# RG-LRU with both directions in one tile, squares on GpSimd, and late gate columns split on GpSimd

## The chip, the cores and the metric

The kernel runs on one core of one Trainium2 chip. The metric is device time in microseconds (us) of one execution; lower is better. The kernel before has a median of 2758.16 us in 3 runs (2757.65 to 2760.92).

## The reference

The program computes two layers (DEPTH = 2) of a hybrid block over 256 context tokens and 512 latent tokens, 1024 channels, in float32. Layer 0 needs all 768 tokens ("full"), layer 1 only the 512 latent ones at its end. One layer, cut to its data flow:

```
h = modulate(rms_norm(x), shift, scale)             # adaLN vectors from c
q, k, v, lx, ly, gdn_qkv, gz, gb, ga, gate = split(h @ w_in)   # 7696 columns
da  = differential attention(q, k, v)               # 4 heads, softmax difference
lru = gelu(ly) * (forward RG-LRU + backward RG-LRU of conv(lx))
gdn = bidirectional gated DeltaNet, chunked
x  += g1 * (sum_i sigmoid(gate_i) * (branch_i @ w_branch_i)) @ w_out
x  += g2 * relu(modulate(rms_norm(x)) @ w1)^2 @ w2
```

The RG-LRU of one direction, which the change touches, is a gated linear scan over time on 512 channels:

```
r, i  = sigmoid(gates of conv(lx))
log_a = -8 * r * softplus(-lam);   a = exp(log_a)
b     = sqrt(-expm1(2 * log_a)) * (i * conv(lx))
h[t]  = a[t] * h[t-1] + b[t]       # direction 1 runs backwards in time
```

## The kernel before

Activations are kept feature-major (128 channels on the partitions, 768 tokens along the free axis). Every large product is done in three passes of a 4-byte type: a weight tile `raw` (128x1024 numbers, 512 KB) is loaded by SyncE's queue, ScalarE copies it rounded to `wh` (the high part), VectorE subtracts to `wl` (the low part, line 174), and TensorE multiplies high by high, high by low and low by high (`mm_feat`, line 201). Three buffers each of `raw`, `wh` and `wl` let the loads run ahead.

A gate column (`fill_gate`, line 863) is one such weight tile: TensorE makes 48 matmuls of it in layer 0 and 24 in layer 1 into one of two large PSUM tiles `pgt`, ScalarE applies a Tanh into `gty`, and the result goes out to HBM. There are 24 gate columns a layer. The first `NG` of them (12 in layer 0, 16 in layer 1) are written in the program ahead of the input projections of the attention and the LRU, the others (12 and 8, here called late) behind the LRU; the scheduler uses them to fill TensorE while other engines work.

The LRU gates are computed earlier and parked in HBM as `lrs[j]`, one tensor for each of four blocks j of 128 channels, with four planes: r of direction 0, i*x of direction 0, r of direction 1, i*x of direction 1. The function `lru` (line 990) takes the blocks in turn. For each direction it loads two planes into a slab `lW` of its own, and calls on ScalarE Exp (a), Tanh (of the same argument, scaled) and Square (a*a); VectorE forms (a*a + 1) * tanh, which is 1 - a*a; ScalarE takes the root, and VectorE or GpSimd multiplies by i*x. Three VectorE scans (forward, backward over the context, backward over the latents) and GpSimd's sum of both directions follow, and a last VectorE product with gelu(ly) (`lys`). ScalarE's calls of `lru` are tied to each other in this order (`behind`), and Exp/Tanh on the one side and Sqrt on the other need different function tables, so an ACT_TABLE_LOAD stands wherever the kind changes.

Behind the LRU come the attention's keys: VectorE writes scaled copies `dkx` (line 1097), TensorE turns them (`pdt`, line 1101), and ScalarE and VectorE split them into `dk`. Then the attention, the merge (`pmf`), the output projection (`pop`) and the MLP (`pm`) follow.

A scheduler places all instructions: it orders each engine's queue before the run, and each engine then works through its own queue in that order. Slabs (11 buffers of 128x3072) are reused as they come free.

Of the kernel before, what the change touches and what calls it, by code (L numbers as in the profile page):

```python
# [22 lines left out]
NG = (12, 16)  # L23
# [5 lines left out]
OFF = {"daq": 0, "dak": 512, "dav": 1024, "lx": 1536, "ly": 2048,  # L29
       "gq": 2560, "gk": 3072, "gv": 3584, "gz": 4096, "ab": 4608, "gate": 4624}  # L30
# [18 lines left out]
def hybrid_prefix_dit_block_kernel(  # L49
# [7 lines left out]
    nc = tc.nc  # L57
    V, S, G, PE = nc.vector, nc.scalar, nc.gpsimd, nc.tensor
# [16 lines left out]
    def slab(name, dt=F32):  # L75
        return sp.tile([P, 3072], dt, name=name, tag="s")
# [48 lines left out]
    for q in range(4):  # L125
        r = slice(32 * q, 32 * q + 16)
# [31 lines left out]
    class Unit:  # L158
        pass

    def wunit(src, early=True):
        u = Unit()
        nk, cols = src.shape[0] // P, src.shape[1]
        with tc.high_priority() if early else nullcontext():
            raw = rp.tile([P, nk, cols], F32, name="raw", tag="raw")
            nc.sync.dma_start(raw, src.rearrange("(k p) c -> p k c", p=P))
            u.h = wp.tile([P, nk, cols], F32R, name="wh", tag="wh")
            u.l = wlp.tile([P, nk, cols], F32R, name="wl", tag="wl")
            u.ins = split(u.h, u.l, raw)
        u.nk = nk  # L170
        return u

    def split(hi, lo, src):
        return S.copy(hi, src), V.tensor_tensor(lo, src, hi.bitcast(F32), op=OP.subtract)  # L174

    class Act:

# [58 lines left out]
    lrs = [dp.tile([P, 4, T], F32, name=f"lrs{i}") for i in range(4)]  # L236
# [626 lines left out]

    def fill_gate(l, L, a, full, n):
        t0, nt = (0, T) if full else (TC, TL)
        us = in_tile(l, OFF["gate"] + P * n)
        ps = big("pgt")
        mm_feat(ps, us, 0, a, pieces(t0, nt))
        y = t3("gty")
        with tc.high_priority():  # L870
            S.activation(y[:, 0:nt], ps[:, 0:nt], AF.Tanh, scale=0.5)  # L871
        nc.sync.dma_start(gts[n][:, t0:T], y[:, 0:nt])
# [32 lines left out]
    def fill_lx_gates(l, L, j, y, weights):  # L905
        wh, wl = weights
        yh, yl = (gp.tile([P, T], F32R, name="gy", tag="g") for _ in range(2))
        parts = ((0, TC, 512, y[:, 0:TC]), (TC, T, 0, y[:, 259:771]))
        for a0, a1, o, src in parts:
            S.copy(yh[:, a0:a1], src)  # L910
            G.tensor_tensor(yl[:, a0:a1], src, yh[:, a0:a1].bitcast(F32), op=OP.subtract)
        for d in range(2):
            for g in range(2):
                ps = big("plg")
                i = 2 * d + g
                for n, (w, x) in enumerate(((wh, yh), (wh, yl), (wl, yh))):
                    for a0, a1, o, src in parts:
                        PE.matmul(ps[:, o:o + a1 - a0], lhsT=w[:, i, :], rhs=x[:, a0:a1], start=(n == 0), stop=(n == 2))
                r = t3("lsg")
                for a0, a1, o, src in parts:  # L920
                    with tc.high_priority():
                        S.activation(r[:, a0:a1], ps[:, o:o + a1 - a0], AF.Tanh, scale=0.5,
                                     bias=L.gb[:, 8 * d + 4 * g + j:8 * d + 4 * g + j + 1])
                    if g == 1:
                        V.scalar_tensor_tensor(r[:, a0:a1], r[:, a0:a1], 1.0, src, op0=OP.add, op1=OP.mult)
                nc.sync.dma_start(lrs[j][:, 2 * d + g, :], r[:, 0:T])

    def fill_ly(l, L, a, full, j):
        t0, nt = (0, T) if full else (TC, TL)
# [65 lines left out]
    def lru(l, L, full, mark):  # L995
        last = [None]
        t0 = 0 if full else TC
        lh = slab("lh").rearrange("p (k t) -> p k t", k=4)

        def act(*args, **kw):  # L1000
            i = S.activation(*args, **kw)
            if last[0] is not None:
                behind(i, last[0])
            last[0] = i

        for j in range(4):
            W = []
            for d in range(2):
                W.append(slab("lW").rearrange("p (k t) -> p k t", k=4))
                after(nc.sync.dma_start(W[d][:, 0:2, :], lrs[j][:, 2 * d:2 * d + 2, :]), mark)  # L1010
            r, ix, at, u = ([W[d][:, i, :] for d in range(2)] for i in range(4))
            for d in range(2):
                c = slice(4 * d + j, 4 * d + j + 1)
                act(at[d], r[d], AF.Exp, scale=L.s8[:, c], bias=L.s8[:, c])
                act(r[d], r[d], AF.Tanh, scale=L.ns8[:, c], bias=L.ns8[:, c])
                act(u[d], at[d], AF.Square)
                V.scalar_tensor_tensor(r[d], u[d], 1.0, r[d], op0=OP.add, op1=OP.mult)
            for d in range(2):
# [323 lines left out]
    for half in range(2):  # L1342
        raws.append([])
        for k in range(8):
# [3 lines left out]
            src = ada_w[0, k * P:(k + 1) * P, 0:2048].rearrange("p (q c) -> p q c", q=2)  # L1348
# [9 lines left out]
    for t in range(6):  # L1358
        xt = xr[t // 3][:, t % 3, :]
        s = slice(t * P, (t + 1) * P)  # L1360
        for hf in range(2):
# [3 lines left out]
            for i in range(4):  # L1365
                n = 4 * hf + i
# [8 lines left out]
    for k in range(8):  # L1375
        i = (G if k % 3 == 1 else V).tensor_tensor(xT[k // 4][:, k % 4, :], x0[k // 4][:, k % 4, :], rb[:, 0:T], op=OP.mult)
# [4 lines left out]
    L = Lay()  # L1381
    spill = [(xs[k // 4][:, k % 4, :], x0[k // 4][:, k % 4, :]) for k in range(8)]
    for l in range(DEPTH):
# [24 lines left out]
        for o in "kvqGLD":  # L1408
# [8 lines left out]
            if o == "L":  # L1417
                lh = lru(l, L, full, R.end)
# [35 lines left out]
        if full:  # L1454
            L = L2
# [36 lines left out]
```

## Time and profile before

| | |
|---|---|
| median of the runs | 2758.16 us |
| profiled execution | 2759.84 us, span 2758.0 us |
| TensorE (PE) busy | 2629.4 us, 95% |
| VectorE (DVE) busy | 1509.1 us, 55% |
| ScalarE (ACT) busy | 1079.5 us, 39% |
| GpSimd (POOL) busy | 456.7 us, 17% |
| share of the chain that ended last | PE 84%, DVE 5%, ACT 5%, issue 3%, DMA 2%, POOL 1% |

How to read it: PE is TensorE's matmuls, PEld its weight loads. The shares are averages over stages that have different limits; a stage has to be read by its own stretch of time. The LRU stage of layer 0 lies at about 600 to 670 us, that of layer 1 at about 2120 to 2185 us. In the rows below, a row of busy times gives the stretch in us, its length, then for each of PE, PEld, DVE, ACT and POOL the busy us and in brackets the number of instructions, then TensorE's granted clock as a share of 2.4 GHz, the DMA engines' share and GB/s. A row of a timeline gives start, duration in us, engine, line, operation, out<-in, shapes, the count that is merged into the row, and in square brackets the idle time before it and what ended it. A row of groups gives line, engine, operation, out<-in and shapes, count, busy us, mean ns of one, and the idle time before.

### The profile page before, as it was taken

To read this page: it belongs to the slowest core of one execution; us is meant where nothing else is said; L and a number is where in the kernel's file an instruction comes from. 1 tells how busy PE (TensorE), PEld (TensorE's weight loads), DVE (VectorE), ACT (ScalarE), POOL (GpSimd) and SP (SyncE) were. 2 spreads that over 40 slices of the span, in tenths; PEclk is the share of its full clock that TensorE was granted. 3 is DMA by queue.
4 is the path that set the end of the run, shared out by engine and by line. 5 is a ranking of instruction groups with operands and counts; after the bars stand their busy time and mean duration, and the time that the engine had idled before them with its cause. 6 is when DMAs were issued, how large, how long until landed. Compare 5 with 4: busy or idle time off the path is not lost.

```text
span 2758.0 us, 44125 instructions
## 1 busy us (share of the span) xinstructions
PE 2629.4 (95%) x17645; PEld 2238.4 (81%) x17645; DVE 1509.1 (55%) x2552; ACT 1079.5 (39%) x1985; POOL 456.7 (17%) x616
## 2 busy tenths in 40 slices
PE   7999999998999989999999989999999798999999
PEld 5788888997888778888888887777897587888887
DVE  6658554459386443333333376686447886544444
ACT  4242454357366233121212253435435764432321
POOL 3001232212012022100001120022222111221100
PEclk9989999999999999999999999999999899999999
DMA  8432233245433643333332222334224533333332
GB/s 277 133 95 88 81 112 102 70 135 182 151 100 104 214 123 115 119 104 122 115 123 77 78 77 70 96 113 148 87 77 129 200 129 120 92 96 99 93 98 77
DMA packets 315588, 318.65 MB, mean 116 GB/s; under 512 B 19500, under 2 KB 268408, under 8 KB 314488
## 3 DMA queue, kind: packets, MB, share of 16 engines
q1 hardware_dynamic: 315384, 315.84, 36.3%
q8 instruction: 139, 2.28, 0.3%
q14 instruction: 65, 0.53, 0.1%
HBM read 259.70 MB, written 56.10 MB: 114 GB/s over the span
## 4 chain that ended last, share of the span: by engine, by line
PE 84%; DVE 5%; ACT 5%; issue 3%; DMA 2%; POOL 1%; SPq 0%; DVEq 0%; ACTq 0%; POOLq 0%
PE pm L201 32%; PE pgt L201 9%; PE pg L201 7%; PE pop L201 4%; PE pqk L218 4%; PE pmf L201 3%; PE pv L218 3%; PE pz L201 2%; PE py L201 2%; PE plx L201 2%; PE pml L201 2%; PE pgd L816 2%; PE ppv L1172 2%; PE pada L347 1%; PE pgd L796 1%
## 5 line engine op out<-in xcount | busy, mean ns | idle before, releaser
L174 ACT CAST wh<-raw 128x1024 fp32r<-128x1024 f32 x288 | 302.3, 1050 | 949.7 <-PE pm L201 616.0
L174 DVE TENSOR_TENSOR wl<-raw,wh 128x1024 fp32r<-128x1024 f32 x288 | 363.8, 1263 | 453.6 <-ACT wh L174 444.8
L201 PE MATMUL pm<-hdh,wh 128*128 128x256 f32 (+1 forms) x896 | 297.4, 332 | 0.4
L201 PE MATMUL pm<-hdl,wh 128*128 128x256 f32 (+1 forms) x896 | 294.5, 329 | 0.0
L201 PE MATMUL pm<-hdh,wl 128*128 128x256 f32 (+1 forms) x896 | 294.3, 328 | 0.0
L1315 DVE SCALAR_TENSOR_TENSOR xT<-pm,mod,xT 128x256 f32<-128x256 f32 (+1 forms) x224 | 133.8, 598 | 236.6 <-PE pm L201 236.6
L201 PE MATMUL pm<-hml,wh 128*128 128x512 f32 (+1 forms) x800 | 244.4, 354 | 5.4 <-DVE hml L459 5.3
L201 PE MATMUL pm<-hmh,wh 128*128 128x512 f32 (+1 forms) x800 | 242.7, 353 | 5.0 <-ACT mr L1296 2.8
L201 PE MATMUL pm<-hmh,wl 128*128 128x512 f32 (+1 forms) x800 | 241.4, 351 | 0.0
L1298 POOL TENSOR_TENSOR mq<-mr 128x768 f32<-128x768 f32 (+1 forms) x64 | 106.5, 1664 | 693.3 <-ACT mr L1296 685.4
L201 PEld LDWEIGHTS pm<-hdh,wh 128*128 128x128 f32 x896 | 170.1, 190 | 30.2 <-DVE xT L1315 7.5
L201 PE MATMUL pgt<-hnh,wh 128*128 128x512 f32 x576 | 177.6, 362 | 7.9 <-ACT gty L871 7.8
L201 PEld LDWEIGHTS pm<-hdh,wl 128*128 128x128 f32 x896 | 170.1, 190 | 15.2
L201 PEld LDWEIGHTS pm<-hdl,wh 128*128 128x128 f32 x896 | 170.2, 190 | 14.8
L201 PE MATMUL pgt<-hnh,wl 128*128 128x512 f32 x576 | 179.7, 364 | 0.0
L201 PE MATMUL pgt<-hnl,wh 128*128 128x512 f32 x576 | 176.7, 361 | 0.0
L201 PEld LDWEIGHTS pm<-hmh,wh 128*128 128x128 f32 x800 | 135.4, 191 | 33.2 <-ACT mr L1296 6.5
L201 PEld LDWEIGHTS pm<-hml,wh 128*128 128x128 f32 x800 | 136.1, 191 | 25.7 <-DVE hml L459 6.2
L201 PEld LDWEIGHTS pm<-hmh,wl 128*128 128x128 f32 x800 | 136.9, 192 | 21.5
L201 PEld LDWEIGHTS pgt<-hnh,wh 128*128 128x128 f32 x576 | 97.2, 193 | 27.0 <-ACT gty L871 10.2
L201 PEld LDWEIGHTS pgt<-hnh,wl 128*128 128x128 f32 x576 | 97.1, 192 | 15.9
L201 PEld LDWEIGHTS pgt<-hnl,wh 128*128 128x128 f32 x576 | 96.2, 191 | 16.0
(427 smaller groups left out, 5963.4 us busy)
## 6 DMA issues: line engine op xcount, KB each, us to landing
raw<-in_mlp_w_dram SPq DMA_DIRECT2D x128, 512.0 KB, 4.1
raw<-in_w_in_dram SPq DMA_DIRECT2D x120, 512.0 KB, 4.1
raw<-in_ada_w_dram SPq DMA_DIRECT2D x80, 512.0 KB, 3.9
lrs<-lsg SPq DMA_DIRECT2D x32, 384.0 KB, 2.4
lW<-lrs SPq DMA_DIRECT2D x16, 768.0 KB, 4.7
raw<-in_w_branch_dram SPq DMA_DIRECT2D x24, 512.0 KB, 4.5
gts<-gty SPq DMA_DIRECT2D x24, 384.0 KB, 2.6
mgg<-gts SPq DMA_DIRECT2D x24, 384.0 KB, 4.2
```

Source lines behind the costliest of these rows:

```text
L174: return S.copy(hi, src), V.tensor_tensor(lo, src, hi.bitcast(F32), op=OP.subtract)
L201: last = PE.matmul(ps[:, o:o + n], lhsT=w, rhs=r[:, t0:t0 + n], start=(k == 0 and i == 0), stop=(k == nk - 1 and i == 2))
L218: PE.matmul(ps[:, 512 * j:512 * j + 256], lhsT=l, rhs=r, start=(k == 0 and i == 0), stop=(k == nk - 1 and i == 2))
L347: i = PE.matmul(ps[32 * q:32 * q + 32, :], lhsT=cact[:, k, :], rhs=two[q // 2][:, 512 * (q % 2):512 * (q % 2) + 512], start=(k == 0), stop ...
L796: i = PE.matmul(dst[32 * h:32 * h + 32, :], lhsT=w, rhs=old[d][:, h, :], start=start, stop=True)
L816: i = PE.matmul(pst[d][h], lhsT=kds[d][r, n % 2, :], rhs=vns[d][r, :], start=True, stop=True)
L1172: PE.matmul(po[:, h * P:(h + 1) * P], lhsT=wt[:, k * P:(k + 1) * P], rhs=R.V[:, k, h * P:(h + 1) * P], start=(k == 0), stop=(k == nk - 1))
L1298: G.tensor_tensor(q[:, 0:nt], r[:, 0:nt], r[:, 0:nt], op=OP.mult)
L1315: V.scalar_tensor_tensor(xv, ps[:, 0:m], L.mod[:, 40 + n, v:v + 1], xv, op0=OP.mult, op1=OP.add)
```

## The change

Three things, with line numbers of the kernel before unless said otherwise.

1. `lrs[j]` gets another order of planes (r of both directions, then i*x of both), so that one transfer brings all four planes into one slab A; a second slab B holds a and a*a of both directions. The two roots of a block become one ScalarE call over 1536 elements.
2. a*a is formed by GpSimd (a product of a with itself) in place of ScalarE's Square: eight in each layer.
3. The low part `wl` of the late gate columns is subtracted by GpSimd in place of VectorE: twelve in layer 0, eight in layer 1.

```
-    def split(hi, lo, src):
-        return S.copy(hi, src), V.tensor_tensor(lo, src, hi.bitcast(F32), op=OP.subtract)
+    def split(hi, lo, src, low=V):
+        return S.copy(hi, src), low.tensor_tensor(lo, src, hi.bitcast(F32), op=OP.subtract)
...
-        us = in_tile(l, OFF["gate"] + P * n)
+        us = in_tile(l, OFF["gate"] + P * n, low=G if n >= NG[l] else V)
...
-                nc.sync.dma_start(lrs[j][:, 2 * d + g, :], r[:, 0:T])
+                nc.sync.dma_start(lrs[j][:, 2 * g + d, :], r[:, 0:T])
...
-            W = []
-            for d in range(2):
-                W.append(slab("lW").rearrange("p (k t) -> p k t", k=4))
-                after(nc.sync.dma_start(W[d][:, 0:2, :], lrs[j][:, 2 * d:2 * d + 2, :]), mark)
-            r, ix, at, u = ([W[d][:, i, :] for d in range(2)] for i in range(4))
+
+            A, B = (slab("lW").rearrange("p (k t) -> p k t", k=4) for _ in range(2))
+            after(nc.sync.dma_start(A, lrs[j]), mark)
             for d in range(2):
                 c = slice(4 * d + j, 4 * d + j + 1)
-                act(at[d], r[d], AF.Exp, scale=L.s8[:, c], bias=L.s8[:, c])
-                act(r[d], r[d], AF.Tanh, scale=L.ns8[:, c], bias=L.ns8[:, c])
-                act(u[d], at[d], AF.Square)
-                V.scalar_tensor_tensor(r[d], u[d], 1.0, r[d], op0=OP.add, op1=OP.mult)
+                act(B[:, d, :], A[:, d, :], AF.Exp, scale=L.s8[:, c], bias=L.s8[:, c])
+                act(A[:, d, :], A[:, d, :], AF.Tanh, scale=L.ns8[:, c], bias=L.ns8[:, c])
+                G.tensor_tensor(B[:, 2 + d, :], B[:, d, :], B[:, d, :], op=OP.mult)
+                V.scalar_tensor_tensor(A[:, d, :], B[:, 2 + d, :], 1.0, A[:, d, :], op0=OP.add, op1=OP.mult)
+            act(A[:, 0:2, :], A[:, 0:2, :], AF.Sqrt)
             for d in range(2):
-                act(r[d], r[d], AF.Sqrt)
-                (V if d else G).tensor_tensor(r[d], r[d], ix[d], op=OP.mult)
-            yl = ix[1]
+                (V if d else G).tensor_tensor(A[:, d, :], A[:, d, :], A[:, 2 + d, :], op=OP.mult)
+            yl = A[:, 3, :]
...
```

The scheduler orders the whole program anew. GpSimd's queue in layer 0's LRU stage, before: `drot` is a leftover of the attention's queries, L1020 the product of the root with i*x, L1028 the sum of both directions.

```order
L981 TENSOR_TENSOR drot<-drot,dsq 128x512 x2
L1020 TENSOR_TENSOR lW<-lW 128x768
L981 TENSOR_TENSOR drot<-drot,dsq 128x512
L1028 TENSOR_TENSOR lh<-lh,lW 128x768
L1020 TENSOR_TENSOR lW<-lW 128x768
L981 TENSOR_TENSOR drot<-drot,dsq 128x512
L1020 TENSOR_TENSOR lW<-lW 128x768
L1028 TENSOR_TENSOR lh<-lh,lW 128x768 x2
```

The same place on GpSimd now. L174 is the low part of a gate column, L1014 the square, L1018 the product (L1020 before), L1026 the sum (L1028 before).

```order
L174 TENSOR_TENSOR wl<-raw,wh 128x1024
L1014 TENSOR_TENSOR lW<-lW 128x768
L981 TENSOR_TENSOR drot<-drot,dsq 128x512
L1014 TENSOR_TENSOR lW<-lW 128x768
L1018 TENSOR_TENSOR lW<-lW 128x768
L981 TENSOR_TENSOR drot<-drot,dsq 128x512
L174 TENSOR_TENSOR wl<-raw,wh 128x1024
L1026 TENSOR_TENSOR lh<-lh,lW 128x768
L174 TENSOR_TENSOR wl<-raw,wh 128x1024
L981 TENSOR_TENSOR drot<-drot,dsq 128x512
L1014 TENSOR_TENSOR lW<-lW 128x768 x2
L174 TENSOR_TENSOR wl<-raw,wh 128x1024
```

Squares and low parts now stand between the products, sums and leftovers, and a low part that TensorE needs can stand behind a sum that waits for VectorE's scans.

ScalarE's queue at the same place, before, from the first table load: L134 is a root of one of the small norms (`oss` of the DeltaNet's output, `dss` of the attention), s and ns mark the LRU's Exp and Tanh, and an L1001 row with neither is a Square or a root.

```order
L134 ACT_TABLE_LOAD
L134 ACTIVATE rsq<-oss 128x24
L1001 ACT_TABLE_LOAD
L1001 ACTIVATE lW<-lW,ns_3985 128x768
L1001 ACTIVATE lW<-lW 128x768
L134 ACT_TABLE_LOAD
L134 ACTIVATE rsq<-dss 128x48
L1001 ACT_TABLE_LOAD
L1001 ACTIVATE lW<-lW,s_3984 128x768
```

The same queue now, from block 0's one root (128x1536) to block 1's first calls.

```order
L1001 ACT_TABLE_LOAD
L1001 ACTIVATE lW<-lW 128x1536
L174 CAST wh<-raw 128x1024
L963 COPY draw<-pqk 128x512
L174 CAST wh<-raw 128x1024
L964 ACTIVATE dsq<-pqk 128x512
L134 ACTIVATE rsq<-dss 128x48
L1001 ACT_TABLE_LOAD
L1001 ACTIVATE lW<-lW,s_3984 128x768
L1001 ACTIVATE lW<-lW,ns_3985 128x768
```

The roots of the small norms now share the table with a root of the LRU or with each other, and block 1's first Exp stands behind the root of the query norms (`dss`).

## Rows read from the trace of the kernel before

**Rows 1.** Busy time of the engines in stretches of layer 0.

```profile
640.00:660.00 20.00, 17.92 (x102) 15.18 (x100) 16.44 (x19) 19.74 (x21) 5.33 (x3) 1.00 0.82 275
660.00:668.00 8.00, 0.78 (x5) 0.78 (x5) 7.04 (x5) 7.93 (x8) 2.90 (x2) 0.59 0.34 103
...
690.00:737.00 47.00, 47.00 (x276) 41.23 (x275) 10.05 (x10) 12.33 (x15) 0.00 (x0) 1.00 0.47 157
```

**Rows 2.** Timeline of TensorE, layer 0, the first key transposes.

```profile
667.22 1.11 PE L1101 MATMUL pdt<-ident,dkx 128*128 128x128 f32 x4 [8.05 <-DVE dkx L1097]
```

**Rows 3.** Groups of ScalarE by line, 599 to 667 us.

```profile
L1001 ACT ACT_TABLE_LOAD x12 | 15.4, 1283 | 0.2
L1001 ACT ACTIVATE lW<-lW 128x768 f32<-128x768 f32 x16 | 13.4, 839 | 4.6 <-DVE lW L1017 4.5
...
L134 ACT ACT_TABLE_LOAD x3 | 3.8, 1283 | 0.1
```

**Rows 4.** Busy time of the engines in stretches of layer 1.

```profile
2150.00:2165.00 15.00, 11.14 (x41) 8.38 (x40) 10.16 (x10) 14.89 (x18) 3.12 (x2) 0.89 0.52 173
2165.00:2180.00 15.00, 6.70 (x32) 4.80 (x30) 13.83 (x15) 12.73 (x16) 5.26 (x2) 0.79 0.59 204
2180.00:2192.00 12.00, 7.67 (x29) 5.54 (x29) 12.00 (x16) 6.50 (x8) 1.26 (x1) 0.50 0.43 149
```

**Rows 5.** Timeline of GpSimd, layer 0.

```profile
632.56 2.57 POOL L1020 TENSOR_TENSOR lW<-lW 128x768 f32<-128x768 f32 x1
...
647.79 1.85 POOL L1020 TENSOR_TENSOR lW<-lW 128x768 f32<-128x768 f32 x1 [9.74 <-issue]
649.60 2.81 POOL L1028 TENSOR_TENSOR lh<-lh,lW 128x768 f32<-128x768 f32 x1
659.29 1.80 POOL L1028 TENSOR_TENSOR lh<-lh,lW 128x768 f32<-128x768 f32 x1 [6.88 <-DVE lW L1026]
```

**Rows 6.** Timeline of VectorE, layer 0.

```profile
618.13 0.95 DVE L1017 SCALAR_TENSOR_TENSOR lW<-lW 128x768 f32<-128x768 f32 x1
619.00 1.75 DVE L1024 TENSOR_TENSOR_SCAN lh<-lW 128x768 f32<-128x768 f32 x1
...
622.71 1.21 DVE L174 TENSOR_TENSOR wl<-raw,wh 128x1024 fp32r<-128x1024 f32 x1
623.85 0.88 DVE L979 TENSOR_TENSOR dsq<-draw,das 128x128 f32<-128x128 f32 x4
624.66 0.68 DVE L1025 TENSOR_TENSOR_SCAN lW<-lW 128x256 f32<-128x256 f32 x1
...
628.50 1.27 DVE L1026 TENSOR_TENSOR_SCAN lW<-lW 128x512 f32<-128x512 f32 x1
...
633.34 1.87 DVE L860 TENSOR_TENSOR gZ<-pot,gZ 128x512 f32<-128x512 f32 x3
...
648.63 2.08 DVE L174 TENSOR_TENSOR wl<-raw,wh 128x1024 fp32r<-128x1024 f32 x1 [1.31 <-ACT wh L174]
650.64 3.38 DVE L1024 TENSOR_TENSOR_SCAN lh<-lW 128x768 f32<-128x768 f32 x1
```

**Rows 7.** Timeline of GpSimd in the MLP: one square alone.

```profile
1064.38 1.47 POOL L1298 TENSOR_TENSOR mq<-mr 128x768 f32<-128x768 f32 x1 [6.15 <-ACT mr L1296]
```

**Rows 8.** Timeline of ScalarE, layer 0.

```profile
599.05 1.03 ACT L1001 ACTIVATE lW<-lW,s 128x768 f32<-128x768 f32 x1 [2.01 <-DMA lW<-lrs]
...
603.55 1.28 ACT L1001 ACT_TABLE_LOAD   x1
604.85 1.03 ACT L1001 ACTIVATE lW<-lW,ns 128x768 f32<-128x768 f32 x1
```

**Rows 9.** Timeline of ScalarE, layer 1, the first Exp.

```profile
2120.59 1.03 ACT L1001 ACTIVATE lW<-lW,s 128x768 f32<-128x768 f32 x1
```

**Rows 10.** Timeline of VectorE, layer 1, the first key copies.

```profile
2170.76 1.29 DVE L1097 TENSOR_TENSOR dkx<-dtok,dr 128x512 f32<-128x512 f32 x2
```

**Rows 11.** DMA issues of the page: count, KB each, us to landing.

```profile
lW<-lrs SPq DMA_DIRECT2D x16, 768.0 KB, 4.7
```

More of the change, by code (lines that the diff above doesn't have):

```diff
@@ L159, in hybrid_prefix_dit_block_kernel, with wunit @@
         pass
-    def wunit(src, early=True):
+    def wunit(src, early=True, low=V):
         u = Unit()
@@ L168, in wunit @@
             u.l = wlp.tile([P, nk, cols], F32R, name="wl", tag="wl")
-            u.ins = split(u.h, u.l, raw)
+            u.ins = split(u.h, u.l, raw, low)
         u.nk = nk
         return u
-    def split(hi, lo, src):
-        return S.copy(hi, src), V.tensor_tensor(lo, src, hi.bitcast(F32), op=OP.subtract)
+    def split(hi, lo, src, low=V):
+        return S.copy(hi, src), low.tensor_tensor(lo, src, hi.bitcast(F32), op=OP.subtract)
     class Act:
@@ L223, in pairs, with in_tile @@
         return t[:, 0:2 * step].rearrange("p (j c) -> p j c", j=2)[:, :, 0:256]
-    def in_tile(l, col, early=True):
-        return [wunit(w_in[l, :, col:col + P], early)]
+    def in_tile(l, col, early=True, low=V):
+        return [wunit(w_in[l, :, col:col + P], early, low)]
     def in_units(l, col):
@@ L1006, in lru @@
         for j in range(4):
-            W = []
-            for d in range(2):
-                W.append(slab("lW").rearrange("p (k t) -> p k t", k=4))
-                after(nc.sync.dma_start(W[d][:, 0:2, :], lrs[j][:, 2 * d:2 * d + 2, :]), mark)
-            r, ix, at, u = ([W[d][:, i, :] for d in range(2)] for i in range(4))
+            A, B = (slab("lW").rearrange("p (k t) -> p k t", k=4) for _ in range(2))
+            after(nc.sync.dma_start(A, lrs[j]), mark)
             for d in range(2):
                 c = slice(4 * d + j, 4 * d + j + 1)
-                act(at[d], r[d], AF.Exp, scale=L.s8[:, c], bias=L.s8[:, c])
-                act(r[d], r[d], AF.Tanh, scale=L.ns8[:, c], bias=L.ns8[:, c])
-                act(u[d], at[d], AF.Square)
-                V.scalar_tensor_tensor(r[d], u[d], 1.0, r[d], op0=OP.add, op1=OP.mult)
+                act(B[:, d, :], A[:, d, :], AF.Exp, scale=L.s8[:, c], bias=L.s8[:, c])
[3 more added lines that the diff above has]
+            act(A[:, 0:2, :], A[:, 0:2, :], AF.Sqrt)
             for d in range(2):
-                act(r[d], r[d], AF.Sqrt)
-                (V if d else G).tensor_tensor(r[d], r[d], ix[d], op=OP.mult)
-            yl = ix[1]
+                (V if d else G).tensor_tensor(A[:, d, :], A[:, d, :], A[:, 2 + d, :], op=OP.mult)
+            yl = A[:, 3, :]
             nc.sync.dma_start(yl[:, t0:T], lys[j][:, t0:T])
-            hs, a1, b1, u1 = lh[:, j, :], at[1], r[1], u[1]
-            V.tensor_tensor_scan(hs, at[0], r[0], 0.0, op0=OP.mult, op1=OP.add)
+            hs, a1, b1, u1 = lh[:, j, :], B[:, 1, :], A[:, 1, :], B[:, 3, :]
+            V.tensor_tensor_scan(hs, B[:, 0, :], A[:, 0, :], 0.0, op0=OP.mult, op1=OP.add)
             V.tensor_tensor_scan(u1[:, TC - 1::-1], a1[:, TC - 1::-1], b1[:, TC - 1::-1], 0.0, op0=OP.mult, op1=OP.add)
```

## The prediction

> **What bounds the kernel now.** I read the page first, then the busy time by stretches, then ScalarE's groups, and last the timelines of VectorE and GpSimd side by side. TensorE is the bound nearly everywhere, so only a stretch in which it stands still can be shortened. In layer 0 it is 2.1 us short of busy in 640 to 660 and does almost nothing in 660 to 668 (0.78 of 8 us), while ScalarE is busy for 27.7 of these 28 us; from 690 on it never stops [rows 1]. That hole ends when VectorE has written the first key copy: the first key transposes start at 667.22 after a wait of 8.05 us [rows 2]. ScalarE is full because of the LRU: fifteen table loads on the lines of the LRU and the small roots, and sixteen Squares and roots of 0.84 us [rows 3]. In layer 1 TensorE lacks 3.9, 8.3 and 4.3 us in the three stretches from 2150 to 2192, 16.5 us together, at a granted clock of 0.89, 0.79 and 0.50, with ScalarE at 14.89 of 15 us in the first of them [rows 4].
>
> The second thing to see is that GpSimd and VectorE hold each other up. GpSimd works from 647.79 to 649.64 and from 649.60 to 652.41 [rows 5]. A low part that VectorE starts at 648.63 takes 2.08 us where one alone takes 1.21, and ends 1.07 us after GpSimd's first instruction; the scan that follows at 650.64 takes 3.38 where 1.75 is usual, and ends 1.61 us after GpSimd's second [rows 6]. Both look like an instruction that stood until GpSimd was done and then ran its full course. Three products with an operand in PSUM at 633.34 take 1.87 us together, 0.62 each, beside a GpSimd instruction that runs from 632.56 to 635.13 [rows 5, 6], so such instructions are not held. GpSimd is held in turn: that product takes 2.57 us where the sum at 659.29 takes 1.80 for the same size.
>
> The Trainium skill states this as a rule (SBUF — State Buffer, section "Who interferes with whom"): a VectorE instruction with two SBUF inputs and a GpSimd instruction that reads SBUF share a port under an exclusive lock, and the later one waits for the whole of the earlier. The trace agrees with it in the four durations above. By the rule the change adds work to a shared resource and the sum is that of the forecast; without it the sum is that of the first rival.
>
> **The change, part by part.** I count what must run on VectorE or GpSimd one at a time, from block 0's first Exp to the first key copy, with the counts from the queues and these prices [rows 5 to 7]. An instruction followed at once by another costs 0.08 us less than it lasts (0.95 at 618.13, the next at 619.00). So VectorE pays 0.87 us for 768 wide, 0.60 for 512 wide, 1.14 for a low part, 1.67 + 0.60 + 1.20 for a block's scans, 0.80 for a group of four small products. GpSimd pays 1.80 for two tensors 768 wide, hence 1.20 for 512, and 1.47 for a square of 768 alone in the MLP. A low part 1024 wide on GpSimd isn't in the trace: 1.80 at least, 2.81 (the longest row) at most, and I take 1.80 x 1024/768 = 2.40.
>
> Layer 0, before: VectorE 13 x 0.87 + 4 x 1.67 + 3 x 1.80 (the other scans of three blocks) + 11 x 0.60 + 3 x 0.80 + 6 x 1.14 (low parts) = 39.2; GpSimd 7 x 1.80 + 3 x 1.20 = 16.2. Together 55.4 of the 68.2 us from 599.05 [rows 8] to 667.22, that is 81%. Now: VectorE 14 x 0.87 + 3 x 3.47 + 11 x 0.60 + 3 x 0.80 = 31.6; GpSimd eight squares 11.8, six products and sums 10.8, three leftovers 3.6, six low parts 14.4, together 40.6. The sum is 72.2 us, more than the stretch had. Packed without a gap that is +4.0 us, at the 81% of before +20.9. I take 95%: ScalarE, which bounded these stages, ran 27.67 of 28 us in layer 0 and 27.62 of 30 in 2150 to 2180 [rows 1, 4], 99% and 92%. That makes 76.0 us, +7.8. TensorE has 14 more gate matmuls ahead of its first key transposes than before, at 47/276 = 0.17 us each [rows 1], which takes back 2.4. Layer 0: **+5.4**, between +1.6 and +18.5.
>
> Layer 1, from 2120.59 [rows 9] to the first key copy at 2170.76 [rows 10], 50.2 us. Before: VectorE 10 x 0.87 + 3 x 3.47 + 7 x 0.60 + 0.80 + 7 x 1.14 = 32.1, GpSimd 3 x 1.80 + 4 x 1.20 = 10.2; 42.3 us, 84%. Now: VectorE 10 x 0.87 + 3 x 3.47 + 6 x 0.60 + 0.80 + 2 x 1.14 = 25.8, GpSimd 11.8 for the squares, six low parts 14.4, and the 10.2; 62.2 us. Without a gap +12.0, at 84% +23.8, at 95% (65.5 us) **+15.3**. The matmuls of gate columns ahead of the transposes are as many as before, so nothing is taken back.
>
> What the change takes off ScalarE is real: in layer 0 eight Squares (6.7 us) and six of the fifteen loads. A load costs 1.30 us: it starts at 603.55 and the next call at 604.85 [rows 8], so six are 7.8 us, 14.5 with the Squares. The Trainium skill (ScalarE: Activation LUTs, section "What ACT_TABLE_LOAD costs") adds a drain of 1.38 us to each load, 2.66 us a switch; by that the six would be worth 16 us. The trace shows no such drain, and I use the row. In layer 1 it is eight Squares and two loads, 9.3 us. I count none of it as a gain, since ScalarE is then no longer what ends last: its root waits for VectorE's product, that one for GpSimd's square, and the square stands behind low parts and sums. If the lock weren't there, all of it would show (first rival).
>
> At nothing I cost three things. The one root of 1536 in place of two of 768 is covered by the waits for its inputs; at worst a block's first direction waits for the second's square and product, 1.47 + 0.87 us a block, which the packing already holds. The one transfer brings the bytes of two; but on SyncE's queue block 1's planes now stand behind block 0's `lys`, which waits for that block's product. Behind it block 1's Exp waits too in layer 0, where it now stands after the root of the query norms, so it is covered; uncovered it would be one landing, 4.7 us a layer [rows 11]. One low part of layer 1 sits in GpSimd's queue inside the DeltaNet's chunk loop: between -1.1 (VectorE relieved) and +2.4, I take 0. The low parts of the last six columns in layer 0 run where TensorE is full and VectorE has room (10.05 of 47 us, [rows 1]).
>
> Sum: +5.4 + 15.3 = +20.7 us on the profiled execution's 2759.84 (span 2758.0 and 1.8 around it), 2780.5. That execution lies 1.7 us above the median of the runs shown, so I forecast **2779 us**. With no gaps in either layer it is +13.6, with the gaps of before +42.3.
>
> **The rivals.** (1) *ScalarE was the bound and its relief shows; faster.* The lock is hidden in the waits that VectorE and GpSimd have anyway. Then the 9.3 us that TensorE lacks in 640 to 668 [rows 1] go, and in layer 1 the 9.3 us that ScalarE is relieved of, out of the 16.5 lacking there [rows 4]: 18.6 us, 2739.6 in the runs' terms. For it: ScalarE is at 99% in these stretches, GpSimd at 5.33 of 20. Against it: the ledger exceeds the stretch. It decides from the point where the added work costs less than the stretches had free: 12.8 us in layer 0 and 7.9 in layer 1, against 16.8 and 19.9 by the rows. (2) *The queues pack as badly as before; slower still.* In layer 0 block 1's Exp now waits for the query norms' root, behind block 0's scans and six more VectorE steps; the low parts wait behind sums, and gate columns starve. Then +42.3, about 2800. (3) *TensorE's filler covers it.* If the gate columns ahead of the key transposes can run on while the LRU is late, the holes don't grow: within 6 us of before, 2758. Against it: only 14 matmuls more stand there in layer 0 and none in layer 1, and their low parts come from the loaded GpSimd.
>
> **How the numbers follow.** Forecast 0.60 (its own range 2768 to 2796), rival 1 0.20, rival 2 0.10, rival 3 0.10. A run of this kernel can tell 0.2%, 5.5 us, from no change. Faster: 0.20 and a tail of rival 3, 0.22. Same: the rest of rival 3, 0.08. Slower: 0.70. The range for 8 in 10 goes from 2746, which holds rival 3 and the weak half of rival 1, to 2803, which holds rival 2.
>
> **What would show it.** ScalarE's Squares and eight table loads gone, GpSimd's busy time up from 456.7 us by 16 x 1.47 + 20 x 2.40 = 71.5 and by waits on top. Right: VectorE's two-input instructions in both stages lengthened by GpSimd's, the first key transposes of layer 0 near 673 to 680 and the first key copy of layer 1 some 15 us later than before, with ScalarE waiting there in place of VectorE. Wrong, if ScalarE is still above 95% busy there, if VectorE's instructions keep their lengths beside GpSimd's squares, or if TensorE's hole at 660 to 668 is closed.

## The result, and the profile after

The changed kernel takes 2785.75 us (median of 3 runs, 2781.22 to 2786.93) against 2758.16: the ratio is 1.0085, 95% interval 1.0066 to 1.0103, about 23 us slower (the two medians as they stand lie 27.6 us apart; the ratio is the figure used below). Its profiled execution took 2781.22 us, 21.4 more than the profiled one of before (2759.84); the forecast for that pair was +20.7. Each experiment below has a median of 4 to 12 runs, which stands beside some 2759.5 us for the kernel before on the same chip; by its ratio the changed kernel would be at 2783 there. Line numbers in rows are those of the kernel that ran.

The busy line of the changed kernel's page (engine, busy us, share of the span, instructions):

```profile
PE 2632.3 (95%) x17645; PEld 2241.3 (81%) x17645; DVE 1538.2 (55%) x2532; ACT 1054.6 (38%) x1951; POOL 538.2 (19%) x652
```

TensorE, with as many matmuls as before, is busy 2.9 us longer (2629.4 before) and idle 18.4 us longer (spans 2779.3 and 2758.0). GpSimd has 81.5 us more than the 456.7 of before. ScalarE has 24.9 less. VectorE lost 20 low parts, some 23 us of work at 1.14 each, and is nevertheless 29.1 us busier than its 1509.1 of before: some 50 us of its busy time is new, and none of it is new work.

Where that time sits can be read in layer 0, from VectorE's timeline (start, duration, engine, line and operation):

```profile
645.06 2.22 DVE L1023 TENSOR_TENSOR_SCAN lW<-lW 128x256 f32<-128x256 f32 x1
647.31 2.31 DVE L1024 TENSOR_TENSOR_SCAN lW<-lW 128x512 f32<-128x512 f32 x1
649.54 2.95 DVE L1022 TENSOR_TENSOR_SCAN lh<-lW 128x768 f32<-128x768 f32 x1
```

and GpSimd's beside it:

```profile
644.11 2.61 POOL L1018 TENSOR_TENSOR lW<-lW 128x768 f32<-128x768 f32 x1 [2.42 <-ACT lW L1001]
646.69 4.19 POOL L1014 TENSOR_TENSOR lW<-lW 128x768 f32<-128x768 f32 x2
```

The three scans take 2.22, 2.31 and 2.95 us where [rows 6] have 0.68, 1.27 and 1.75. The short one starts at 645.06, seems to stand until GpSimd's product ends at 646.72 and ends 0.56 us after it. The long one starts at 649.54, and ends 1.61 us after the second square, which ends at 650.88. GpSimd pays too: the two squares take 4.19 us, not the 2 x 1.47 of [rows 7]. The engines take turns, as in [rows 5, 6], only oftener.

TensorE's stretches in layer 0, columns as in [rows 1] (stretch, its length, then busy us of PE, PEld, DVE, ACT and POOL, granted clock, DMA), the changed kernel's four and then 668 to 690 of the kernel before:

```profile
640.00:660.00 20.00, 20.00 (x115) 17.37 (x114) 16.82 (x9) 14.75 (x14) 15.89 (x7) 1.00 0.50 166
660.00:668.00 8.00, 4.42 (x18) 3.17 (x16) 7.96 (x5) 5.66 (x6) 5.19 (x4) 0.84 0.98 336
668.00:690.00 22.00, 11.66 (x58) 9.81 (x58) 21.93 (x18) 7.93 (x10) 12.27 (x5) 0.67 0.31 92
690.00:737.00 47.00, 47.00 (x283) 41.44 (x282) 13.92 (x16) 13.97 (x19) 12.08 (x5) 1.00 0.44 150
```

```profile
668.00:690.00 22.00, 22.00 (x131) 19.63 (x130) 19.34 (x26) 8.96 (x14) 2.21 (x1) 0.92 0.38 117
```

```profile
675.92 1.11 PE L1099 MATMUL pdt<-ident,dkx 128*128 128x128 f32 x4 [8.07 <-DVE dkx L1095]
```

ScalarE, 19.74 of 20 us in 640 to 660 before, now has 14.75, and GpSimd went from 5.33 to 15.89. TensorE's hole hasn't closed; it has moved into 660 to 690, and the first key transposes start at 675.92, again after 8.07 us of waiting, in place of 667.22 [rows 2]. At TensorE's first MLP matmul (1017.34 before, 1025.57 now) layer 0 has cost 8.2 us, at GpSimd's first square of the MLP (1046.25 and 1055.70) 9.5.

ScalarE's groups from 599 to 676 us (busy us, mean ns, then idle time in front and what ended it), which answer to [rows 3]:

```profile
L1001 ACT ACT_TABLE_LOAD x8 | 10.3, 1283 | 0.1
...
L1001 ACT ACTIVATE lW<-lW 128x1536 f32<-128x1536 f32 x4 | 5.9, 1487 | 12.2 <-DVE lW L1015 12.2
...
L134 ACT ACT_TABLE_LOAD x1 | 1.3, 1283 | 0.0
L134 ACT ACTIVATE rsq<-dss 128x48 f32<-128x48 f32 x2 | 0.5, 236 | 12.5 <-DVE dss L1084 12.5
```

Nine table loads are left of fifteen, and the Squares are gone. ScalarE now stands 12.2 us before its four roots and 12.5 before the query norms' root, each time for VectorE.

Layer 1, the stretches that answer to [rows 4] and the one behind them, and the two ends of the LRU's stretch:

```profile
2150.00:2165.00 15.00, 12.97 (x58) 10.40 (x56) 10.64 (x6) 9.76 (x10) 11.54 (x6) 1.00 0.97 368
2165.00:2180.00 15.00, 10.92 (x38) 8.81 (x39) 13.54 (x7) 9.05 (x10) 10.46 (x5) 0.77 0.48 143
2180.00:2192.00 12.00, 2.63 (x12) 1.86 (x10) 11.80 (x7) 8.13 (x10) 8.66 (x4) 0.83 0.59 220
2192.00:2215.00 23.00, 12.56 (x44) 8.71 (x45) 23.00 (x29) 12.00 (x14) 4.14 (x2) 0.50 0.23 80
```

```profile
2127.26 1.03 ACT L1001 ACTIVATE lW<-lW,s 128x768 f32<-128x768 f32 x1 [0.33 <-DMA lW<-lrs]
```

```profile
2190.51 2.35 DVE L1095 TENSOR_TENSOR dkx<-dtok,dr 128x512 f32<-128x512 f32 x2
```

From the first Exp to the first key copy it is 63.25 us, against 50.17 before [rows 9, 10]: +13.1. TensorE lacks 9.4 of 12 us ahead of the copy, and runs at a granted clock of 0.50 behind it (2192 to 2215; 0.88 in the kernel before). The first softmax Exp of the layer comes 20.7 us later than before (2206.43, now 2227.17), of which 6.7 were there at the LRU's first Exp.

### The profile page after: what moved, and what is told of

Read it like the earlier page. It is cut to its first block, busy times and chain, and to the rows that moved or that the text cites. A ratio compares the mean times of both kernels' runs of the same rounds, so it can differ in the third digit from the quotient of the medians.

```text
span 2779.3 us, 44091 instructions
## 1 busy us (share of the span) xinstructions
PE 2632.3 (95%) x17645; PEld 2241.3 (81%) x17645; DVE 1538.2 (55%) x2532; ACT 1054.6 (38%) x1951; POOL 538.2 (19%) x652
## 4 chain that ended last, share of the span: by engine, by line
PE 83%; DVE 6%; DMA 3%; issue 3%; ACT 3%; POOL 1%; SPq 0%; DVEq 0%; ACTq 0%; POOLq 0%
PE pm L201 32%; PE pgt L201 9%; PE pg L201 7%; PE pqk L218 4%; PE pop L201 4%; PE pmf L201 3%; PE pv L218 3%; PE plx L201 2%; PE pz L201 2%; PE py L201 2%; PE pgd L816 2%; PE pml L201 1%; PE ppv L1170 1%; PE pada L347 1%; PE pgd L796 1%
## 5 line engine op out<-in xcount | busy, mean ns | idle before, releaser
L174 ACT CAST wh<-raw 128x1024 fp32r<-128x1024 f32 x288 | 302.2, 1049 | 949.2 <-PE pm L201 615.9
L174 DVE TENSOR_TENSOR wl<-raw,wh 128x1024 fp32r<-128x1024 f32 x268 | 335.6, 1252 | 450.1 <-ACT wh L174 441.7
L201 PEld LDWEIGHTS pm<-hdh,wl 128*128 128x128 f32 x896 | 170.1, 190 | 15.2
```

Of the source, the lines that this page charges most:

```text
L174: return S.copy(hi, src), low.tensor_tensor(lo, src, hi.bitcast(F32), op=OP.subtract)
L201: last = PE.matmul(ps[:, o:o + n], lhsT=w, rhs=r[:, t0:t0 + n], start=(k == 0 and i == 0), stop=(k == nk - 1 and i == 2))
```

## The experiments

**The four corners.** The theory is the port: VectorE's instructions with two SBUF inputs and GpSimd's reading ones run one at a time, and the change adds to that queue. Its rivals: the order (the query norms' root now stands in front of block 1's Exp, and ScalarE waits 12.5 us for it), and the layout (one slab, one transfer, one root). The first three runs put back one part, the other, and both; the fourth gives the squares to VectorE.

E1, low parts back on VectorE:

```diff
-        us = in_tile(l, OFF["gate"] + P * n, low=G if n >= NG[l] else V)
+        us = in_tile(l, OFF["gate"] + P * n, low=V)
```

> All low parts back on VectorE, the squares stay on GpSimd, slab and single root as in the changed kernel. Port theory (VectorE and GpSimd take turns on two-input work from SBUF): the ledger is 64.6 us in layer 0 and 54.6 in layer 1; at the 95 to 98% at which the changed kernel packs, layer 0 is back at its old length and layer 1 is 5 to 7 us over: +5 to +7 us on the kernel before, 2763 to 2765. Order theory (the query norms' root ahead of block 1's Exp, which stands behind it again here): layer 0 is back as well, but layer 1 keeps its +14: about +14. Layout theory (one root, one transfer, one slab make the loss): no change against the changed kernel, about +21 to +27.

Measured: 2769.4 us, ratio 1.0032 (1.0019 to 1.0044).

E2, squares back on ScalarE:

```diff
-                G.tensor_tensor(B[:, 2 + d, :], B[:, d, :], B[:, d, :], op=OP.mult)
+                act(B[:, 2 + d, :], B[:, d, :], AF.Square)
```

> Squares back on ScalarE, the late low parts stay on GpSimd, slab and single root as in the changed kernel; the query norms' root stays ahead of block 1's Exp. Port theory: ledger 60.4 and 50.4 us; layer 0 fits into its old length, layer 1 is 1 to 3 us over: 0 to +3 us on the kernel before. Order theory: layer 0 keeps its loss, +7 at least. Layout theory: +21 to +27.

Measured: 2771.05 us, 1.0038 (1.0026 to 1.0051).

E3, both edits together:

> Squares back on ScalarE and low parts back on VectorE: only the slab, the single transfer and the single root of 1536 are left of the change. Port theory: ledger 52.8 and 42.8 us, about that of before; ScalarE bounds again and has ten table loads fewer, 10 x 1.30 = 13 us, of which the part in the TensorE holes shows: 5 to 10 us faster than before. Layout theory: as slow as the changed kernel, +21 to +27. Order theory: the root stands behind block 1's Exp again, so no loss: 0 to -10.

Measured: 2761.19 us, 1.0000 (0.9990 to 1.0010).

E4, the first edit of E1, and the squares on VectorE:

```diff
-                G.tensor_tensor(B[:, 2 + d, :], B[:, d, :], B[:, d, :], op=OP.mult)
+                V.tensor_tensor(B[:, 2 + d, :], B[:, d, :], B[:, d, :], op=OP.mult)
```

> Squares on VectorE (0.87 us each in place of 1.47 on GpSimd), low parts on VectorE, slab and single root as in the changed kernel. Port theory: ledger 59.8 and 49.8 us, against 64.6 and 54.6 with the squares on GpSimd: layer 0 fits, layer 1 is 0.6 to 2 us over, -4 to +2 us on the kernel before and 4 to 8 faster than with the squares on GpSimd. If VectorE and GpSimd did not hold each other up, VectorE would have 7 us a layer more to do and GpSimd nothing less in the way: slower than with the squares on GpSimd by up to 14.

Measured: 2761.17 us, 1.0001 (0.9992 to 1.0010).

The layout theory falls: with both parts back nothing of the loss is left. By the ratios each part alone costs 9 to 10.5 us, both together 23; with the low parts on VectorE, the squares cost nothing there and 8 us on GpSimd. Three expectations missed. E1 was to lie 5 to 7 us over the kernel before, and lies 9.9 over it. E2 should have fitted into the stretch and cost at most 3 us; and E3, with ten table loads fewer than before, should have been 5 to 10 us faster.

**Is it the port, or the chain?** On GpSimd a square takes longer and the product waits for it; that would slow the chain without any port. So E5 adds GpSimd work to E3 that nothing in the chain waits for, and E6 as much GpSimd time that reads nothing:

```diff
                 V.scalar_tensor_tensor(A[:, d, :], B[:, 2 + d, :], 1.0, A[:, d, :], op0=OP.add, op1=OP.mult)
+                G.tensor_tensor(B[:, 2, :], B[:, d, :], B[:, d, :], op=OP.mult)      # E5
+                G.memset(B[:, 2, :], 0.0)                                            # E6, twice
```

> Base is the kernel with both parts back (slab, one transfer and one root only; 2761 us). Added to it, per direction, one spare GpSimd product 768 wide that reads the Exp's result and writes a plane nobody reads (16 in all, 1.47 us each alone). Nothing in the LRU's chain waits for it. Port theory (VectorE's two-input instructions stand while GpSimd reads): 11.8 us a layer of shared time as with the squares on GpSimd, so 5 to 10 us slower than the base, 2766 to 2771, with VectorE's scans beside it stretched. Chain theory (the squares cost only because the product waits for a slower engine): 2761 within 3 us. A behaviour of the Trainium skill (SBUF - State Buffer, section 'Who interferes with whom') is what the port theory rests on.

Measured: 2774.56 us, 1.0053 (1.0037 to 1.0068), 13.4 us over E3, more than the 5 to 10 expected.

> Same base. Added per direction: two spare GpSimd memsets 768 wide into the same plane, some 0.74 us each (estimate from 0.53 us for 512 and 1.81 for 2048 in the trace of before), so GpSimd is busy about as long as with the spare products, but reads nothing. If what VectorE waits for is GpSimd's reading: 2761 within 3 us, VectorE's scans beside the memsets keep 1.74 us. If it is any use of SBUF by GpSimd, or GpSimd's queue being full: as slow as with the spare products, 2766 to 2771.

Measured: 2760.32 us, 0.9998 (0.9988 to 1.0009).

The busy lines of the two pages, E5 and then E6:

```profile
PE 2632.1 (95%) x17645; PEld 2240.5 (81%) x17645; DVE 1533.3 (55%) x2552; ACT 1064.9 (38%) x1967; POOL 485.9 (18%) x632
```

```profile
PE 2631.2 (95%) x17645; PEld 2237.6 (81%) x17645; DVE 1516.0 (55%) x2552; ACT 1065.4 (39%) x1967; POOL 480.2 (17%) x648
```

VectorE runs the same 2552 instructions in both, and takes 17.3 us longer beside the products. The order of the queues is no rival here: in both LRU stages (560 to 740 and 2080 to 2240 us) ScalarE's and VectorE's order is the same in E5 and E6, but for three or four single rows that one of the two traces has and the other lacks. Block 1 of layer 1, VectorE in E5 and GpSimd beside it:

```profile
2151.80 0.96 DVE L1015 SCALAR_TENSOR_TENSOR lW<-lW 128x768 f32<-128x768 f32 x1 [4.03 <-ACT lW L1001]
2153.66 1.73 DVE L174 TENSOR_TENSOR wl<-raw,wh 128x1024 fp32r<-128x1024 f32 x1 [0.90 <-ACT wh L174]
2155.32 2.21 DVE L1015 SCALAR_TENSOR_TENSOR lW<-lW 128x768 f32<-128x768 f32 x1
```

```profile
2152.84 3.88 POOL L1016 TENSOR_TENSOR lW<-lW 128x768 f32<-128x768 f32 x2 [6.93 <-DVE lW L1015]
```

The same three instructions in E6, and GpSimd's memsets:

```profile
2140.98 0.96 DVE L1015 SCALAR_TENSOR_TENSOR lW<-lW 128x768 f32<-128x768 f32 x1 [2.23 <-ACT lW L1001]
2142.84 1.23 DVE L174 TENSOR_TENSOR wl<-raw,wh 128x1024 fp32r<-128x1024 f32 x1 [0.90 <-ACT wh L174]
2144.50 0.96 DVE L1015 SCALAR_TENSOR_TENSOR lW<-lW 128x768 f32<-128x768 f32 x1 [0.44 <-ACT lW L1001]
```

```profile
2142.00 0.75 POOL L1016 MEMSET lW<- 128x768 f32 x1 [5.11 <-DVE lW L1015]
2142.80 0.74 POOL L1017 MEMSET lW<- 128x768 f32 x1
2143.60 0.75 POOL L1016 MEMSET lW<- 128x768 f32 x1
2144.41 0.74 POOL L1017 MEMSET lW<- 128x768 f32 x1
```

Beside memsets the low part takes 1.23 and the product 0.96; beside reads 1.73 and 2.21, and the pair of reads takes 3.88, not 2.94. This is shown by a run, and not only argued: what costs is GpSimd's reading of SBUF, since neither GpSimd's busy time nor anyone's wait for its result does. The Trainium skill (SBUF — State Buffer, section "Who interferes with whom") has the same distinction: a VectorE instruction with two SBUF inputs contends with a GpSimd instruction that reads SBUF, "not with one that only writes it". E6 agrees with that half, E5 with the other.

**The order.** E10 moves one instruction of the changed kernel, layer 0's query-norm root, behind block 1's Exps and Tanhs:

```diff
+            if j == 1:
+                L.b1 = last[0]                 # block 1's second Tanh
             act(A[:, 0:2, :], A[:, 0:2, :], AF.Sqrt)
...
+                behind(i, mark)                # in rsqrt; mark is L.b1 for the queries of layer 0
```

> The changed kernel with one thing moved: in layer 0 the query norms' root is put behind block 1's two Exps and Tanhs on ScalarE, where the kernel before has it about. In the changed kernel ScalarE stands 12.5 us in front of it. Order theory: a good part of the 9 us that layer 0 loses comes back, 2774 to 2779. Port theory: what ends layer 0's stage is the shared work of VectorE and GpSimd, which is as much as before: 2783 within 3 us, and ScalarE waits elsewhere instead.

Measured: 2783.66 us, 1.0091 (1.0077 to 1.0105). ScalarE's timeline in E10, and TensorE's stretch 617 to 690 in the changed kernel and in E10:

```profile
625.16 1.03 ACT L1003 ACTIVATE lW<-lW,s 128x768 f32<-128x768 f32 x1 [6.43 <-DMA lW<-lrs]
...
630.54 0.24 ACT L134 ACTIVATE rsq<-dss 128x48 f32<-128x48 f32 x1
...
670.82 1.49 ACT L1003 ACTIVATE lW<-lW 128x1536 f32<-128x1536 f32 x1 [8.32 <-DVE lW L1017]
```

```profile
617.00:690.00 73.00, 53.16 (x283) 44.99 (x281) 69.54 (x58) 38.73 (x42) 50.20 (x22) 0.84 0.54 180
```

```profile
617.00:690.00 73.00, 53.82 (x286) 45.99 (x285) 70.12 (x57) 40.97 (x43) 50.47 (x22) 0.84 0.55 182
```

Block 1's Exp comes 8.8 us earlier (625.16 for 633.98, now after 6.43 us of waiting for its planes), and the 12.5 us wait is gone. The first key transposes come 8.7 us earlier too, at the time they had before the change:

```profile
667.22 1.11 PE L1103 MATMUL pdt<-ident,dkx 128*128 128x128 f32 x4 [9.67 <-DVE dkx L1099]
```

Yet TensorE is as idle in the stretch as in the changed kernel, ScalarE waits 8.32 us before the last root instead, TensorE's first MLP matmul comes only 1.9 us earlier (1023.71), and the run's time is the same. The order theory falls. ScalarE's longest wait in this stretch was worth nothing; that it is only where the shared queue's delay surfaces is the likely reading. And the start of the key transposes does not measure what layer 0 loses.

**The transfer.** E3 brought no gain from its ten loads. Its SyncE queue in layer 1 shows block 1's planes (L1009) behind block 0's `lys` (L1020), and ScalarE the landing:

```profile
2135.96 0.34 SPq L1020 DMA_DIRECT2D lW<-lys  x1
2136.35 0.42 SPq L1009 DMA_DIRECT2D lW<-lrs  x1
```

```profile
2144.07 1.03 ACT L1001 ACTIVATE lW<-lW,s 128x768 f32<-128x768 f32 x1 [2.05 <-DMA lW<-lrs]
```

E7 is E3 with that one issue moved ahead, E8 the same on E4, E9 the same on the changed kernel:

```diff
+        ahead = planes(0)                      # slabs A, B and the transfer into A
         for j in range(4):
-            A, B = (slab("lW").rearrange("p (k t) -> p k t", k=4) for _ in range(2))
-            after(nc.sync.dma_start(A, lrs[j]), mark)
+            A, B = ahead
...
             yl = A[:, 3, :]
+            if j < 3:
+                ahead = planes(j + 1)
             nc.sync.dma_start(yl[:, t0:T], lys[j][:, t0:T])
```

> Base with both parts back, and the next block's transfer of gate planes is put on SyncE's queue ahead of this block's lys. In the base, block 1's Exp of layer 1 starts at 2144.07 after waiting for its planes, 21.9 us after block 0's; in the kernel before it is 14.2 us after. If the queue's order is what costs layer 1 there: block 1's Exp of layer 1 some 4 to 8 us earlier, and 2 to 5 us faster than the base, 2756 to 2759. If the base is bound elsewhere (VectorE, or the granted clock): 2761 within 2 us.

Measured: 2752.84 us, 0.9968 (0.9957 to 0.9980), 8.3 us under E3, where 2 to 5 were expected. SyncE and ScalarE in E7:

```profile
2122.39 1.54 SPq L1008 DMA_DIRECT2D lW<-lrs  x1
```

```profile
2135.05 1.02 ACT L1001 ACTIVATE lW<-lW,s 128x768 f32<-128x768 f32 x1
```

Block 1's Exp stands 12.5 us behind block 0's (2122.54) in place of 21.9, and from there to the first softmax Exp layer 1 takes 80.9 us in place of 89.4. E7 is 6.7 us faster than the kernel before, within the 5 to 10 that were expected of E3.

> Squares and low parts on VectorE, and the next block's transfer ahead of this block's lys. Same reasoning on the base with the squares on VectorE (2761): 2756 to 2759 if the queue's order costs layer 1; 2761 within 2 us if not. A candidate for a version faster than before.

Measured: 2762.32 us, 1.0011 (1.0000 to 1.0021). No gain, 9.5 us behind E7; layer 1 keeps 88.2 us between those two points. With the planes in time, squares on VectorE cost what they did not cost before. The lengths of layer 1's stretch, first Exp to first key copy, fit a full shared queue: E3's ledger of 42.8 us fills 51.2 us in E3 and 43.6 in E7, E4's of 49.8 fills 54.8 in E4 and 51.6 in E8 (84, 98, 91 and 96%). In E3 the squares still found a gap, in E7 none. These are estimates by the prediction's prices; no run tests this reading.

> The changed kernel (0.85% slower than before, 2783 us beside these runs of before) with the next block's planes put on SyncE's queue ahead of this block's lys. In the changed kernel block 1's Exp of layer 1 waits 3.02 us for its planes and stands 23.8 us after block 0's. If the transfer's place costs here as it did with both parts back (8.3 us): 2774 to 2777. If the port binds there whatever ScalarE does, the wait was covered: 2783 within 2 us. As predicted (covered in layer 0, in layer 1 not more than one landing of 4.7 us): -0 to -5.

Measured: 2781.47 us, 1.0081 (1.0067 to 1.0094), within 2 us of the changed kernel's 2783. Layer 1 has block 1's planes in time (its Exp at 2148.35, 18.2 us behind block 0's, was 23.8), and the root behind it waits 6.92 us in place of 4.06:

```profile
2148.35 1.02 ACT L1001 ACTIVATE lW<-lW,s 128x768 f32<-128x768 f32 x1
...
2162.07 1.48 ACT L1001 ACTIVATE lW<-lW 128x1536 f32<-128x1536 f32 x1 [6.92 <-DVE lW L1019]
```

From the first Exp to the first softmax Exp layer 1 takes 96.9 us, 3.0 less than in the changed kernel; the run's time does not show them. In layer 0 E9 goes further than E10. Block 1's Exp stands there ahead of the query norms' root and waits for no planes, 15 us earlier than in the changed kernel, and TensorE's stretch is no fuller:

```profile
618.97 1.03 ACT L1001 ACTIVATE lW<-lW,s 128x768 f32<-128x768 f32 x1
```

```profile
617.00:690.00 73.00, 53.02 (x279) 45.24 (x278) 69.48 (x56) 41.01 (x43) 51.38 (x22) 0.81 0.49 159
```

**The other way.** If GpSimd's reads cost, the LRU's remaining ones do too. E11 is E7 with the products on VectorE; E12 moves the sums as well:

```diff
-                (V if d else G).tensor_tensor(A[:, d, :], A[:, d, :], A[:, 2 + d, :], op=OP.mult)
+                V.tensor_tensor(A[:, d, :], A[:, d, :], A[:, 2 + d, :], op=OP.mult)
...
-            G.tensor_tensor(hs[:, t0:T], hs[:, t0:T], u1[:, t0:T], op=OP.add)     # E12 only
+            V.tensor_tensor(hs[:, t0:T], hs[:, t0:T], u1[:, t0:T], op=OP.add)
```

> Both parts back and the planes first (2752.8 us), and the four products a layer that GpSimd does (root times input, 1.80 us) go to VectorE (0.87). By the port's ledger the shared time falls by 0.93 each, 3.7 us a layer: 0 to 6 us faster, 2747 to 2753. If VectorE is a bound by itself and GpSimd's work costs nothing there: VectorE has 3.5 us a layer more, slower by up to 7.

Measured: 2745.67 us, 0.9952 (0.9939 to 0.9964), 7.2 us under E7.

> As the kernel with the products on VectorE, and the sums of the two directions on VectorE too (0.87 for 1.80 in layer 0, 0.60 for 1.20 in layer 1): GpSimd has nothing left in the LRU. By the ledger another 3.7 us of shared time less in layer 0 and 2.4 in layer 1: 0 to 5 us faster than with the products alone, 2745 to 2752. If VectorE is a bound by itself: slower than that by up to 6.

Measured: 2741.77 us, 0.9937 (0.9925 to 0.9950): 3.9 us under E11, 17.8 us faster than the kernel before and 41 faster than the changed one. Both lie below the expected ranges. Of the 17.8 us E7's layout and transfer made 6.7 and the moves to VectorE 11.1. The two moves also shorten the LRU's chain, so they don't separate the port from it; E5 and E6 do. The busy line of E12, and its stretch 617 to 690:

```profile
PE 2630.2 (96%) x17645; PEld 2238.6 (82%) x17645; DVE 1508.6 (55%) x2568; ACT 1062.3 (39%) x1965; POOL 423.3 (15%) x600
```

```profile
617.00:690.00 73.00, 70.78 (x417) 61.82 (x416) 65.57 (x84) 49.62 (x58) 2.66 (x2) 0.98 0.65 222
```

VectorE runs 16 instructions more than before and is busy 0.5 us less. TensorE is short of busy by 2.2 us in the stretch, where the changed kernel lacks 19.8.

## Why the prediction was right

**The bound.** Right, and now shown: the time went where VectorE and GpSimd take turns (E5 against E6), not to the order (E10) or the layout (E3). The rival in which ScalarE's relief shows is out: with the transfer in its way E3 gains nothing, in the changed kernel ScalarE waits, and E9 gives ScalarE its data 5.6 us earlier for no gain in the run's time. Its 18.6 us showed in no run; the most that the layout gave without GpSimd's added reads was E7's 6.7 (ratio 0.9968). That ScalarE's relief is worth nothing at all is not shown: E1 and E5 have the same sixteen products on GpSimd, and E1, in which they replace ScalarE's Squares, is some 5 us faster (ratios 1.0032 and 1.0053). The filler rival is out too, since the hole grew.

**Layer 0, +5.4.** The ledger's 72.2 us were to take 76.0; from 599.55 (the old first Exp plus the 0.5 us by which the stretch began late) to 675.92 they took 76.4, and packed to 95%, as chosen. As they ran, GpSimd had a seventh product, at 672.81, in front of the transposes, where the ledger had six products and sums: 74.0 us, 97%. The price of a low part on GpSimd, an estimate of 2.40 us, measured 2.41 (at 601.08). The step that failed is the 2.4 us that fourteen more gate matmuls were to take back: layer 0 stands at +8.7 at its first key transposes, at +8.2 at TensorE's first MLP matmul and at +9.5 at GpSimd's first square, so nothing, or 0.5 us, came back there. Taking the first key copy for the end of the hole was a weak point as well: in E10 the transposes start as early as before the change, and layer 0 still loses 6.4 us by its first MLP matmul. Between that layer's last MLP product (+9.9) and the first Exp of layer 1 (+6.7) some 3 us return; no run tells why.

**Layer 1, +15.3.** The stretch grew by 13.1: 62.2 us of work in 63.25, 98% and not 95% (some 61 us, 97%, as they ran, since one of the six low parts came ahead of the first Exp). By the first softmax Exp it is 14.1.

**The sum.** It came out at +21.4 in the profiled pair against +20.7, because layer 0's term was too small by about what returned later. The mechanism held, but that the sum is so close is luck. The median of the runs lies 6.8 us above the 2779 forecast.

**The ledger as a rule.** The sum was right because the stretches were full. As a threshold, under which added work is free, the ledger is wrong, and E2 showed it: 60.4 and 50.4 us, which fit, cost 10.5 us and not 0 to 3. By the same prices the runs compare as follows (both columns in us):

| pair | more shared time by the ledger | more run time |
|---|---|---|
| E2 over E3 | 15.2 | 9.9 |
| E5 over E3 | 23.5 | 13.4 |
| changed kernel over E1 | 15.2 | 13.6 |
| E7 over E11 | 7.4 | 7.2 |
| E11 over E12 | 6.1 | 3.9 |
| changed kernel over E2 | 23.6 | 12.0 |
| E8 over E7 | 14.0 | 9.5 |
| E1 over E3 | 23.6 | 8.2 |
| E4 over E3 | 14.0 | 0.0 |

That is 0.5 to 1.0 us of run time for each us in seven of the nine pairs, 0.35 and nothing in the last two. In the last four the run with more shared time also has sixteen Squares less on ScalarE, which may make up for a part. By the ledger E3's stretch of layer 1 is 84% full (42.8 of 51.2 us) and E2's 93% (50.4 of 54.3): of the work added, 3.1 us went into the length although gaps were there. That an instruction that stands delays the chain behind it, wherever else the queue has room, is the likely reason; no run shows it by itself.

**ScalarE's relief at nothing.** Right for the changed kernel as far as E9 and E10 show. Ten loads went, not eight (46 before, 36 after).

**What was costed at nothing.** The transfer behind `lys` is covered in the changed kernel, as said, but for the 3 us of layer 1 that E9 shows. With both parts back it costs 8.3 us (E3 against E7), all of it in layer 1; with the squares on VectorE it costs nothing (E4 against E8). The price of 4.7 us for a landing was that of half the bytes [rows 11]; the single transfer of 1536 KB lands after 7.7:

```profile
lW<-lrs SPq DMA_DIRECT2D x8, 1536.0 KB, 7.7
```

The low parts of the last six columns in layer 0 were free: TensorE has its 47.00 of 47 us from 690 to 737 with GpSimd at 12.08. The wait for the query norms' root appeared as the second rival had it, and cost nothing (E10). GpSimd's busy time rose by 81.5 us, of which 71.5 is the work by the prediction's prices and the rest, as it seems, waiting.

## What to carry to other kernels

Before moving an instruction to an idle GpSimd, ask whether it reads SBUF and whether VectorE runs two-input SBUF instructions in the same stretch: then it is not idle, but at the head of VectorE's queue, and here each us of shared time cost 0.5 to 1.0 us in most of the pairs of runs. In such a stretch count both engines as one, and try the opposite move: VectorE does each of the LRU's products and sums in half of GpSimd's time, and moving them there gained 11.1 us. A long wait of a third engine is no measure of what removing it brings: two moves that removed 12.5 and 5.6 us of ScalarE's delay left the run's time as it was.

## What the runs showed of the hardware that was not expected

Size doesn't protect. In the changed kernel, VectorE's small root steps of 24 elements stand behind two low parts on GpSimd. GpSimd's timeline, then VectorE's:

```profile
2121.95 1.33 POOL L981 TENSOR_TENSOR drot<-drot,dsq 128x512 f32<-128x512 f32 x1 [2.67 <-issue]
2123.24 4.73 POOL L174 TENSOR_TENSOR wl<-raw,wh 128x1024 fp32r<-128x1024 f32 x2
```

```profile
2122.17 1.15 DVE L847 TENSOR_SCALAR oss<-oss 128x24 f32<-128x24 f32 x1
2123.61 0.61 DVE L137 RECIPROCAL rsq<-rsq 128x24 f32<-128x24 f32 x2 [0.29 <-ACT rsq L134]
2124.14 3.90 DVE L138 SCALAR_TENSOR_TENSOR rsq<-rsq 128x24 f32<-128x24 f32 x2
2127.97 0.17 DVE L139 TENSOR_TENSOR rsq<-rsq,oss 128x24 f32<-128x24 f32 x1
```

The two L138 steps take 3.90 us (one took 0.18 at 604.53 in the kernel before) and end as the low parts do (2128.04 and 2127.97), while the reciprocals with one input run through beside the first of them. The TENSOR_SCALAR, also with one input, took 1.15 us beside a GpSimd sum that ran from 2121.95 to 2123.28, where the same step took 0.17 in the kernel before, beside no GpSimd instruction (2116.80). So one input does not free every operation.

The runs of one kernel spread by as much as an edit is worth, and the granted clock goes with them: E3's eleven runs go from 2753.82 us at a mean clock of 0.979 to 2766.87 at 0.974. Two profiles alone can't show a difference of a few us.
